# Inverting 16x16 triangular blocks on VectorE: substitution in blocks of 4 and two doublings in place of plain substitution

## The chip, the cores and the metric

The kernel runs on one core of one Trainium2 chip. The metric is the device time of one execution in microseconds (us), taken as the median of several executions. One further execution is recorded by the hardware profiler. Its engines are called PE (TensorE matmuls), PEld (TensorE weight loads), DVE (VectorE), ACT (ScalarE), POOL (GpSimd) and SP (the engine that issues most DMAs).

## What is computed

The reference is a two-layer decoder on 512 tokens of width 1024: a gated-DeltaNet layer, a differential-attention layer, and an MLP behind each. The change lies in the first layer's delta rule, which has 8 heads. For each head and chunk of tokens the reference does this:

```python
a_mat = where(strict, einsum('bhnik,bhnjk->bhnij', kb, kc) * decay, 0.0)   # strictly lower triangular
sol = triangular_solve(eye + a_mat, rhs, left_side=True, lower=True, unit_diagonal=True)
u, w = sol[..., :DV], sol[..., DV:]
...
v_new = u_i - w_i @ state          # step by step over the chunks
o_i = qg_i @ state + qk_i @ v_new
state = state * gl_i + kd_i.T @ v_new
```

What matters here is the inverse of a unit lower triangular matrix I + A, needed before the recurrence over the chunks can run.

## The kernel before, in words

The kernel computes the whole trunk in one program. Every large product is three fp32r matmuls on split operands (lines 300, 301 and 302 in `three`): weights are loaded as `raw`, ACT rounds them to `wh` (line 293), and DVE or POOL forms the remainder `wl` (line 284). During the delta-rule layer DVE forms `wl`; later POOL does.

The layer handles the heads in one Python loop. `proj_head(h)` does the projections of q, k and v on PE into three PSUM banks `pj` (their pool has three), and `conv_silu` empties each bank: one ACT pass (line 481) and three DVE passes (line 483). A bank is free for the next head's matmuls when the third pass has run. `gdn(h)` is a generator in three parts; the loop runs the first two parts of head h and then the last of head h-1.

The part that the change touches is in the first part of `gdn`. The head is worked in four units of 128 tokens. `bq` (line 558) holds the unit's triangular matrix and the attention weights. Lines 570 and 574 cut out the 16x16 diagonal blocks (8 in each unit, 32 in all) into `dc`. Two DMAs from SP (lines 576 and 578) bring them through DRAM into `mt`, which holds one block on each of 32 partitions, 256 numbers each, transposed: `mt[p, s, r]` is row r, column s. POOL sets `xv` to 32 unit matrices (line 581).

Then 15 steps of substitution follow. Step s takes column s of the block times the finished part of row s of the inverse into `pr` (line 584), and subtracts that from the rows below (line 586). Both are DVE instructions on (15 - s) x (s + 1) numbers on each of 32 partitions: 15, 28, 39, 48, 55, 60, 63, 64 and back down, 680 in all for each of the two lines, and each instruction needs the one before it. Two more DMAs (lines 589 and 591) bring the inverses back as `tc`; line 593 spreads them into the block-diagonal `t`; PE transposes `t` (line 598), and the inverse of the whole 128x128 matrix is completed by doubling from 16 to 32, 64 and 128 with matmuls on PE and copies and subtractions on DVE (lines 605 to 638). The recurrence (lines 670 to 690) needs that.

The order in which instructions stand on each engine is not the order of the program's text. The build fixes it for each engine, and mixes the steps of one head with the work of its neighbours; at run time each engine takes its queue strictly in that order, waiting on semaphores. While head h is being inverted, the convolutions of head h+1 or h+2, the `wl` remainders of coming weights, the recurrence of head h-1 and the modulation products of line 193 stand between its steps on DVE. After the last head come the output gates (`gate`, line 711 on), then the output projection.

Of the kernel before, what the change touches and what calls it, by code (L numbers as in the profile page):

```python
# [10 lines left out]
F32 = mybir.dt.float32  # L11
F32R = mybir.dt.float32r
AF = mybir.ActivationFunctionType
ALU = mybir.AluOpType
AX = mybir.AxisListType
# [5 lines left out]
S = 512  # L21
# [8 lines left out]
SUB = 16  # L30
# [55 lines left out]
def trunk_kernel(ctx: ExitStack, tc: tile.TileContext, a, outT):  # L86
    nc = tc.nc
    V, G, A, T = nc.vector, nc.gpsimd, nc.scalar, nc.tensor
# [3 lines left out]
    def nm(s):  # L92
        count[0] += 1
        return f"{s}_{count[0]}"

    def open_pool(name, side="left", bufs=1):
        st = ExitStack()
        p = st.enter_context(tc.tile_pool(name=nm(name), bufs=bufs, side=side, reuse_waits="tile"))
        return p, st
# [40 lines left out]
    def v3(ap, n=P):  # L140
        return ap.rearrange("p (u f) -> p u f", f=n)
# [286 lines left out]
    g_pool, g_st = open_pool("g", "right")  # L428
# [10 lines left out]
    def gt_(name):  # L439
# [18 lines left out]
                           op0=ALU.mult, op1=ALU.mult)  # L458
# [42 lines left out]
    def uu(t, n):  # L501
        return t[:, n * P:(n + 1) * P]

    def m4(ap):
        return ap.unsqueeze(1).to_broadcast([P, 4, P])

    m_sub = mask[:, M_L1:M_L1 + P]

    def gdn(h):
        def natural(src, tag="a"):  # L510
            ps = bank(tag)
            for c in range(NT):
                T.transpose(uu(ps, c), uu(src, c), ident)
            return ps
# [35 lines left out]
        for n in range(2):  # L550
# [5 lines left out]
            for c in (2 * n, 2 * n + 1):  # L556
                o = (c % 2) * 256
                V.scalar_tensor_tensor(out=v3(bq[n][:, o:o + 256]), in0=v3(ps[:, o:o + 256]), scalar=sj[:, c:c + 1],
                                       in1=uu(ex, c).unsqueeze(1).to_broadcast([P, 2, P]), op0=ALU.mult, op1=ALU.mult)
# [9 lines left out]
        for n in range(2):  # L569
            V.tensor_tensor(out=v3(db[:, n * 256:(n + 1) * 256]),  # L570
                            in0=bq[n].rearrange("p (u t f) -> p u t f", u=2, t=2)[:, :, 0, :],
                            in1=m_sub.unsqueeze(1).to_broadcast([P, 2, P]), op=ALU.mult)
# [4 lines left out]
        mt = g_pool.tile([32, SUB, SUB], F32, tag="mt", name=nm("mt"), bufs=2)  # L577
        nc.sync.dma_start(mt.rearrange("p r c -> p (r c)"), d1.rearrange("u (b r) c -> (u b) (r c)", r=SUB))
        xv = g_pool.tile([32, SUB, SUB], F32, tag="xv", name=nm("xv"), bufs=2)
        pr = g_pool.tile([32, SUB, SUB], F32, tag="pr", name=nm("pr"), bufs=2)  # L580
        G.tensor_copy(xv, eye)
        for s in range(SUB - 1):
            shp = [32, SUB - 1 - s, s + 1]
            V.tensor_tensor(out=pr[:, s + 1:, :s + 1], in0=mt[:, s, s + 1:].unsqueeze(2).to_broadcast(shp),
                            in1=xv[:, s, :s + 1].unsqueeze(1).to_broadcast(shp), op=ALU.mult)
            V.tensor_tensor(out=xv[:, s + 1:, :s + 1], in0=xv[:, s + 1:, :s + 1], in1=pr[:, s + 1:, :s + 1],
                            op=ALU.subtract)
        d2 = dp.tile([32, SUB * SUB], F32, tag="d2", name=nm("d2"))
        nc.sync.dma_start(d2, xv.rearrange("p r c -> p (r c)"))
        tc_ = g_pool.tile([P, 4, SUB], F32, tag="tc", name=nm("tc"), bufs=2)  # L590
# [3 lines left out]
                        in0=tc_.unsqueeze(2).to_broadcast([P, 4, P // SUB, SUB]),  # L594
                        in1=m4(m_sub).rearrange("p u (b c) -> p u b c", c=SUB), op=ALU.mult)
# [20 lines left out]
        for b in (32, 64):  # L616
# [13 lines left out]
            if b == 32:  # L630
                p0, p1 = parts[0]
                for n in range(4):
# [3 lines left out]
                                in1=v3(pz[p1, 0:4 * b], b), op=ALU.subtract)  # L636
            for p0, p1 in parts:
                V.tensor_tensor(out=v3(z)[p0, :, p1], in0=v3(z)[p0, :, p1], in1=v3(pz[p0, 0:4 * b], b),
                                op=ALU.subtract)
# [27 lines left out]
        for c in range(NT):  # L667
            r = uu(vn, 0)
            if c > 0:
# [3 lines left out]
                else:  # L673
# [3 lines left out]
                                       op0=ALU.mult, op1=ALU.add)  # L677
# [28 lines left out]
        else:  # L706
            V.scalar_tensor_tensor(out=oT[h], in0=natural(o, "r"), scalar=cc(C_OUTG), in1=sz[h],
                                   op0=ALU.mult, op1=ALU.mult)
# [20 lines left out]
    for h in range(H):  # L729
        proj_head(h)  # L730
        heads.append(gdn(h))
        next(heads[h])
        next(heads[h])
        if h:
            next(heads[h - 1], None)
# [50 lines left out]
    def after0(sl, rb):  # L786
        rbs.append(rb)
        for k in range(KT):
# [19 lines left out]
                           op0=ALU.add, op1=ALU.subtract)  # L808
# [202 lines left out]
```

## Time and profile before

| what | value |
|---|---|
| median of 3 runs | 1384.9 us (1381.57 to 1387.92) |
| the profiled execution | 1381.92 us, its span 1380.1 us, granted TensorE clock 0.986 |
| busy over the span | PE 1309.7 us, DVE 850.9 us, ACT 529.1 us, POOL 471.4 us |
| the inversions' stage, 100 to 346 us | PE 226.1 us of 246, DVE 221.6 us of 246 |
| lines 584 and 586 (15 of each in each of 8 heads) | 240 DVE instructions, first at 106.3 us, last at 346.0 us |

The profile is read as follows. Busy time counts an instruction's whole run, so neighbours in a pipelined engine overlap; the time that an instruction takes from its engine's queue is better read as the distance between its start and the next one's start. A timeline row that ends in "x2" holds two instructions. The granted clock is the share of full speed that the throttle allowed TensorE.

### The profile page before, as it was taken

What the parts mean: (1) busy time and instruction counts of PE and PEld (TensorE: products, weight loads), DVE (VectorE), ACT (ScalarE), POOL (GpSimd) and SP (SyncE); (2) the same over time, 40 slices, a digit from 0 to 9 for tenths busy, and PEclk for the clock granted to TensorE, in tenths of its full rate; (3) what the DMA queues carried; (4) which work ended last, traced back from release to release, by engine and by line L of the source; (5) the groups of instructions that cost most, each with busy time, mean ns of one, the idle gap of its engine ahead of it and who ended that gap; (6) DMA issues with size and microseconds to landing.
All of it is one profiled execution on the core that took longest, in us unless ns stands there. A gap on an engine that the chain in (4) does not pass through costs nothing. (4 is left out here: it accounts for less than half of the span.)

```text
span 1380.1 us, 19204 instructions
## 1 busy us (share of the span) xinstructions
PE 1309.7 (95%) x7240; PEld 1101.4 (80%) x7240; DVE 850.9 (62%) x1688; ACT 529.1 (38%) x951; POOL 471.4 (34%) x281
## 2 busy tenths in 40 slices
PE   4887998999999999999999999999999999999997
PEld 3665787777789888888888987888798888888886
DVE  6989899899846987778861687777552110031113
ACT  3394344443424533225332354444344322143221
POOL 3324132222004544444444012232135444444441
PEclk9997999999999999999999999999999999999998
DMA  9632223225542776776753233222113233233221
GB/s 314 212 90 57 81 78 81 74 72 147 175 151 65 266 239 225 242 236 219 241 165 100 81 100 104 65 66 66 61 62 123 92 96 103 92 100 99 92 76 62
DMA packets 113212, 174.97 MB, mean 127 GB/s; under 512 B 16384, under 2 KB 56992, under 8 KB 113120
## 3 DMA queue, kind: packets, MB, share of 16 engines
q1 hardware_dynamic: 112416, 172.92, 39.5%
q8 instruction: 57, 0.93, 0.3%
q10 hardware_dynamic: 704, 0.83, 0.2%
q14 instruction: 35, 0.29, 0.1%
HBM read 170.04 MB, written 2.62 MB: 125 GB/s over the span
## 5 line engine op out<-in xcount | busy, mean ns | idle before, releaser
L284 POOL TENSOR_TENSOR wl<-raw,wh 128x1024 fp32r<-128x1024 f32 (+1 forms) x137 | 329.3, 2404 | 392.9 <-ACT wh L293 392.9
L293 ACT ACTIVATE wh<-raw 128x1024 fp32r<-128x1024 f32 (+2 forms) x217 | 216.0, 996 | 502.0 <-PE pj L301 250.1
L300 PE MATMUL pj<-h,wh 128*128 128x512 f32 (+1 forms) x816 | 290.9, 360 | 16.0 <-ACT h L278 5.5
L301 PE MATMUL pj<-h,wh 128*128 128x512 f32 (+1 forms) x816 | 292.6, 359 | 0.0
L302 PE MATMUL pj<-h,wl 128*128 128x512 f32 (+1 forms) x816 | 290.4, 358 | 1.1 <-DVE wl L284 1.1
L193 DVE SCALAR_TENSOR_TENSOR mw<-mw,one,cs 128x1024 f32<-128x1024 f32 x96 | 210.1, 2202 | 47.5 <-ACT one L213 47.2
L300 PEld LDWEIGHTS pj<-h,wh 128*128 128x128 f32 x816 | 155.9, 192 | 37.2 <-ACT h L278 7.5
L302 PEld LDWEIGHTS pj<-h,wl 128*128 128x128 f32 x816 | 156.6, 192 | 19.4 <-DVE wl L284 2.4
L301 PEld LDWEIGHTS pj<-h,wh 128*128 128x128 f32 x816 | 156.9, 192 | 17.9 <-DVE h L279 0.3
L301 PE MATMUL pj<-u,wh 128*128 128x512 f32 (+1 forms) x448 | 160.9, 359 | 0.0
L302 PE MATMUL pj<-u,wl 128*128 128x512 f32 (+1 forms) x448 | 160.9, 359 | 0.0
L300 PE MATMUL pj<-u,wh 128*128 128x512 f32 (+1 forms) x448 | 160.8, 359 | 0.0
L346 DVE SCALAR_TENSOR_TENSOR x<-pj,mod,x 128x256 f32<-128x256 f32 (+1 forms) x53 | 30.2, 584 | 152.2 <-PE pj L302 152.2
L284 DVE TENSOR_TENSOR wl<-raw,wh 128x1024 fp32r<-128x1024 f32 (+2 forms) x80 | 84.5, 1058 | 18.7 <-ACT wh L293 18.6
L300 PEld LDWEIGHTS pj<-u,wh 128*128 128x128 f32 x448 | 84.6, 189 | 12.7 <-issue 0.2
L301 PEld LDWEIGHTS pj<-u,wh 128*128 128x128 f32 x448 | 84.6, 189 | 12.5
L302 PEld LDWEIGHTS pj<-u,wl 128*128 128x128 f32 x448 | 84.6, 189 | 12.5
L767 DVE SCALAR_TENSOR_TENSOR pj<-pj,r 128x512 f32<-128x512 f32 x32 | 21.6, 690 | 52.2 <-ACT r L766 52.0
L301 PE MATMUL pn<-h,wh 128*128 128x512 f32 x128 | 49.8, 389 | 0.0
L300 PE MATMUL pn<-h,wh 128*128 128x512 f32 x128 | 49.8, 389 | 0.0
L300 PE MATMUL pm<-h,wh 128*128 128x512 f32 x128 | 49.8, 389 | 0.0
L302 PE MATMUL pm<-h,wl 128*128 128x512 f32 x128 | 49.8, 389 | 0.0
(298 smaller groups left out, 2371.7 us busy)
## 6 DMA issues: line engine op xcount, KB each, us to landing
raw<-in_mlp_w_dram SPq DMA_DIRECT2D x128, 512.0 KB, 3.7
mw<-in_mod_wT_dram SPq DMA_DIRECT2D x96, 512.0 KB, 4.7
raw<-in_a_w_in_dram SPq DMA_DIRECT2D x96, 128.0 KB, 2.6
mw<-in_kv_mod_wT_dram SPq DMA_DIRECT2D x16, 512.0 KB, 5.1
raw<-in_kv_w_dram SPq DMA_DIRECT2D x16, 512.0 KB, 3.3
x<-in_xT_dram SPq DMA_DIRECT2D x16, 256.0 KB, 6.0
raw<-in_a_w_in_dram SPq DMA_DIRECT2D x16, 256.0 KB, 2.9
raw<-in_a_w_out_dram SPq DMA_DIRECT2D x8, 512.0 KB, 4.3
```

The source lines that it names most:

```text
L193: V.scalar_tensor_tensor(out=w, in0=w, scalar=one, in1=cs, op0=ALU.mult, op1=ALU.mult, accum_out=raw_mod[:, c:c + 1])
L284: (V if n else G).tensor_tensor(out=out, in0=x, in1=hi.bitcast(F32), op=ALU.subtract)
L293: A.activation(wh, raw, AF.Copy)
L300: T.matmul(ps, lhsT=wh, rhs=xh, start=first, stop=False, skip_group_check=skip)
L301: T.matmul(ps, lhsT=wh, rhs=xl, start=False, stop=False, skip_group_check=skip)
L302: T.matmul(ps, lhsT=wl, rhs=xh, start=False, stop=last, skip_group_check=skip)
L346: V.scalar_tensor_tensor(out=x[d][:, sl], in0=ps[j][:, sl], scalar=mod[:, gt + d:gt + d + 1], in1=x[d][:, sl], op0=ALU.mult, op1=ALU.add)
L767: V.scalar_tensor_tensor(out=ps[j], in0=ps[j], scalar=0.0, in1=r, op0=ALU.max, op1=ALU.mult)
```

## The change

`blocks_inv(mt, xv)` takes the place of the 15 steps. It first negates `mt` (one instruction on 256 numbers a partition). Substitution then runs on the four 4x4 diagonal blocks at once: three steps of two instructions, on 12, 16 and 12 numbers. Then pairs of neighbouring inverses are doubled, X21 = X22 (-M21) X11. Each of the two products in that is a multiply that writes all b x b x b terms into `pr`, and a reduction over the last axis. From 4 to 8 there are two such pairs, one after the other (64 terms each); from 8 to 16 there is one (512 terms). In all there are 1 + 6 + 8 + 4 = 19 instructions for 30. Each part needs the one before it. `pr` has one buffer of 512 numbers where it had two of 256, and a small tile `tq` is new.

```diff
+    def at(t, off, *dims):
+        v = t[:]
+        return bass.AP(tensor=v.tensor, offset=v.offset + off, ap=[list(v.ap[0])] + [list(d) for d in dims])
+
+    def blocks_inv(mt, xv):
+        V.tensor_scalar(out=mt, in0=mt, scalar1=-1.0, scalar2=None, op0=ALU.mult)
+        b, q = 4, 4 * (SUB + 1)
+        for i in range(b - 1):
+            m = b - 1 - i
+            pr = g_pool.tile([32, S], F32, tag="pr", name=nm("pr"), bufs=1)
+            prod, rest = at(pr, 0, (16, 4), (i + 1, m), (1, i + 1)), at(xv, (i + 1) * SUB, (q, 4), (SUB, m), (1, i + 1))
+            V.tensor_tensor(out=prod, in0=at(mt, i * SUB + i + 1, (q, 4), (1, m), (0, i + 1)),
+                            in1=at(xv, i * SUB, (q, 4), (0, m), (1, i + 1)), op=ALU.mult)
+            V.tensor_tensor(out=rest, in0=rest, in1=prod, op=ALU.add)
+        for b in (4, 8):
+            for lo in range(0, SUB, 2 * b):
+                d = lo * (SUB + 1)
+                pr = g_pool.tile([32, S], F32, tag="pr", name=nm("pr"), bufs=1)
+                tq = g_pool.tile([32, 64], F32, tag="tq", name=nm("tq"), bufs=1)
+                prod = at(pr, 0, (b * b, b), (b, b), (1, b))
+                V.tensor_tensor(out=prod, in0=at(mt, d + b, (1, b), (0, b), (SUB, b)),
+                                in1=at(xv, d, (0, b), (1, b), (SUB, b)), op=ALU.mult)
+                V.tensor_reduce(out=at(tq, 0, (b, b), (1, b)), in_=prod, axis=AX.X, op=ALU.add)
+                V.tensor_tensor(out=prod, in0=at(xv, d + b * (SUB + 1), (SUB, b), (0, b), (1, b)),
+                                in1=at(tq, 0, (0, b), (1, b), (b, b)), op=ALU.mult)
+                V.tensor_reduce(out=at(xv, d + b * SUB, (SUB, b), (1, b)), in_=prod, axis=AX.X, op=ALU.add)
...
-        pr = g_pool.tile([32, SUB, SUB], F32, tag="pr", name=nm("pr"), bufs=2)
         G.tensor_copy(xv, eye)
-        for s in range(SUB - 1):
-            shp = [32, SUB - 1 - s, s + 1]
-            V.tensor_tensor(out=pr[:, s + 1:, :s + 1], in0=mt[:, s, s + 1:].unsqueeze(2).to_broadcast(shp),
-                            in1=xv[:, s, :s + 1].unsqueeze(1).to_broadcast(shp), op=ALU.mult)
-            V.tensor_tensor(out=xv[:, s + 1:, :s + 1], in0=xv[:, s + 1:, :s + 1], in1=pr[:, s + 1:, :s + 1],
-                            op=ALU.subtract)
+        blocks_inv(mt, xv)
```

In the new text the four instructions of a doubling are lines 532 (multiply), 534 (reduce), 535 (multiply) and 537 (reduce); the negation is line 517, the small steps are lines 523 and 525. Lines behind the function have moved by 24, those of `gdn` ahead of the call by 30 (598 is now 622, 574 is now 604).

The change moves instructions on every engine, since the build lays out the order anew. The first place is DVE's queue at head 6 (the seventh). Before, the last third of its substitution stands between the next head's `bq` passes, single steps between single foreign instructions:

```order
L586 TENSOR_TENSOR xv_2810<-xv_2810,pr_2811 32x6x10
L558 SCALAR_TENSOR_TENSOR bq_3168<-pa_3176,sj_3164,ex_3147 128x256
L676 SCALAR_TENSOR_TENSOR r_2569<-pr_2560,neg,vn_2544 128x128
L584 TENSOR_TENSOR pr_2811<-mt_2808,xv_2810 32x5x11
L558 SCALAR_TENSOR_TENSOR bq_3168<-pa_3176,sj_3164,ex_3147 128x256
L586 TENSOR_TENSOR xv_2810<-xv_2810,pr_2811 32x5x11
L570 TENSOR_TENSOR db_3183<-bq_3167,mask 128x256
```

Now the same head's last doubling stands there, four long instructions between steps of head 5's recurrence (`st`, `o`, `r`, `y`):

```order
L532 TENSOR_TENSOR pr_2816<-mt_2790,xv_2792 32x512
L714 SCALAR_TENSOR_TENSOR st_2540<-st_2540,eg_all,pr_2542 128x128
L534 TENSOR_REDUCE tq_2817<-pr_2816 32x64
L550 TENSOR_REDUCE sqk_3138<-sqk_3136 128x4
L684 TENSOR_TENSOR o_2541<-o_2541,pr_2542 128x128
L700 SCALAR_TENSOR_TENSOR r_2575<-pr_2542,neg,vn_2526 128x128
L535 TENSOR_TENSOR pr_2816<-xv_2792,tq_2817 32x512
L571 TENSOR_SCALAR sqk_3138<-sqk_3138 128x4
L705 COPY y_2579<-pr_2542 128x128
L537 TENSOR_REDUCE xv_2792<-pr_2816 32x8x8
```

From a head's first to its last instruction on `xv` there were 66, 81, 110, 92, 89, 93, 84 and 75 rows of DVE's queue for heads 0 to 7; now there are 40, 46, 61, 60, 50, 53, 50 and 44.

The second place is PE's queue at the transposes of the same head's `t`. Before, they stand among the matmuls of an output gate, with the transposes of head 5's finished output (line 513) just ahead of them:

```order
L513 MATMUL pr_2614<-mask,o_2176 128x128 x4
L301 MATMUL pj_3474<-h_175,wh_3496 128x512
L302 MATMUL pj_3474<-h_174,wl_3498 128x512
L300 MATMUL pj_3475<-h_172,wh_3496 128x512
L598 MATMUL pi_2849<-mask,t_2847 128x128 x4
L605 MATMUL pi_2856<-t_2847,bq_2785 128x128 x2
```

Now they stand behind fewer matmuls, with transposes of the next head (line 543) ahead of them:

```order
L543 MATMUL pa_3286<-mask,cv_3104 128x128 x4
L301 MATMUL pj_3360<-h_183,wh_3423 128x512
L302 MATMUL pj_3360<-h_182,wl_3425 128x512
L300 MATMUL pj_3361<-h_180,wh_3423 128x512
L301 MATMUL pj_3361<-h_181,wh_3423 128x512
L622 MATMUL pi_2828<-mask,t_2826 128x128 x4
L629 MATMUL pi_2835<-t_2826,bq_2767 128x128 x2
```

Counted in projection matmuls that stand ahead of them on PE, the transposes of heads 0 to 7 stood behind 264, 312, 376, 460, 528, 611, 667 and 753; now they stand behind 280, 320, 339, 433, 519, 570, 645 and 728.

## Prediction

> **What bounds the kernel now.** I read the page first. Its engine line, and the rows that cut the span into 40 slices of 34.5 us, say that TensorE sets the time, and when VectorE is near its own limit:
>
> ```profile
> PE 1309.7 (95%) x7240; PEld 1101.4 (80%) x7240; DVE 850.9 (62%) x1688; ACT 529.1 (38%) x951; POOL 471.4 (34%) x281
> PE   4887998999999999999999999999999999999997
> DVE  6989899899846987778861687777552110031113
> PEclk9997999999999999999999999999999999999998
> ```
>
> PE is busy for 1309.7 of 1380.1 us. DVE's 62% is a mean: in slices 2 to 10, where the heads are inverted, its digits are 8 and 9, later 1 to 8. PE's digits of 8 lie there too. So I asked for the busy time of each engine by stretches of that stage (columns: stretch, its length, PE, PEld, DVE, ACT, POOL with instruction counts, granted clock, DMA share, GB/s):
>
> ```profile
> 100.00:140.00 40.00, 31.23 (x169) 24.66 (x168) 37.02 (x117) 19.15 (x34) 18.46 (x14) 0.75 0.25 60
> 140.00:220.00 80.00, 77.50 (x533) 63.05 (x533) 71.33 (x222) 36.36 (x63) 21.57 (x18) 1.00 0.28 77
> 220.00:300.00 80.00, 72.43 (x502) 59.62 (x503) 72.30 (x202) 37.75 (x68) 19.21 (x16) 0.98 0.29 79
> 300.00:346.00 46.00, 44.96 (x330) 35.85 (x329) 40.99 (x135) 13.65 (x29) 8.81 (x5) 1.00 0.44 123
> 346.00:380.00 34.00, 32.65 (x214) 25.91 (x213) 28.44 (x58) 14.99 (x29) 2.78 (x2) 1.00 0.59 180
> ```
>
> From 100 to 346 us PE is busy for 226.1 of 246 us and DVE for 221.6: two engines at about 90% that feed each other. PE is idle for 19.9 us, DVE for 24.4. Where DVE is fullest (93% of the first 40 us) PE is emptiest (8.8 us idle), and the granted clock is 0.75 there. The waits of PE in that stage, and those of DVE, name the direction (columns: total us, times, longest):
>
> ```profile
> PE pi L598 <- DVE t L593: 5.5, 4, 2.6
> PE pj L300 <- DVE cv L483: 4.5, 3, 2.6
> PE pj L300 <- DVE pr L584: 2.7, 1, 2.7
> ...
> DVE um L624 <- PE pi L622: 8.2, 11, 1.1
> DVE sj L545 <- POOL rk L543: 3.6, 7, 0.8
> ```
>
> PE waits for 12.7 of its 19.9 idle us in these three rows, all on DVE: for the spread inverses, and for PSUM banks that the convolutions empty late because they queue on DVE. DVE waits mostly for short round trips to PE.
>
> **The steps removed.** Three pieces of DVE's timeline give prices by the distance from one start to the next (start us, run us, what):
>
> ```profile
> 120.25 0.31 DVE L584 TENSOR_TENSOR pr<-mt,xv 32x60 f32<-32x60 f32 x2
> 120.50 0.31 DVE L586 TENSOR_TENSOR xv<-xv,pr 32x60 f32<-32x60 f32 x2
> 120.74 0.32 DVE L584 TENSOR_TENSOR pr<-mt,xv 32x55 f32<-32x55 f32 x2
> 120.98 0.32 DVE L586 TENSOR_TENSOR xv<-xv,pr 32x55 f32<-32x55 f32 x2
> 121.23 0.32 DVE L584 TENSOR_TENSOR pr<-mt,xv 32x48 f32<-32x48 f32 x2
> 121.47 0.32 DVE L586 TENSOR_TENSOR xv<-xv,pr 32x48 f32<-32x48 f32 x2
> 121.72 0.32 DVE L584 TENSOR_TENSOR pr<-mt,xv 32x39 f32<-32x39 f32 x2
> 121.96 0.32 DVE L586 TENSOR_TENSOR xv<-xv,pr 32x39 f32<-32x39 f32 x2
> 122.21 0.17 DVE L584 TENSOR_TENSOR pr<-mt,xv 32x28 f32<-32x28 f32 x1
> ```
>
> ```profile
> 284.73 0.16 DVE L586 TENSOR_TENSOR xv<-xv,pr 32x15 f32<-32x15 f32 x1
> 284.81 0.17 DVE L584 TENSOR_TENSOR pr<-mt,xv 32x15 f32<-32x15 f32 x1
> 284.89 0.67 DVE L284 TENSOR_TENSOR wl<-raw,wh 128x512 fp32r<-128x512 f32 x1
> ```
>
> ```profile
> 99.01 1.02 DVE L574 TENSOR_REDUCE dc<-db 128x64 f32<-128x512 f32 x1
> 99.96 0.67 DVE L520 TENSOR_REDUCE sqq<-sqk 128x4 f32<-128x512 f32 x1
> 100.55 0.73 DVE L483 SCALAR_TENSOR_TENSOR cv<-pj,cols,cv 128x511 f32<-128x511 f32 x1
> ```
>
> A step on 15 numbers takes 0.08 us of the queue, the plain reduction of 512 (line 520) takes 0.59. So a number costs (0.59 - 0.08)/497 = 1.03 ns, and an instruction 0.065 us besides. As a check, between 120.25 and 122.21 stand 16 steps on 60, 55, 48 and 39 numbers, 0.1225 us each, where the formula gives 0.117. A head's 30 steps with 1360 numbers cost 30 x 0.065 + 1.40 = 3.35 us, eight heads 26.8 us.
>
> **The steps added.** Line 574 is the useful row: it too reduces 512 to 64, reading with an innermost step of 16 numbers, and takes 0.95 us, 1.73 ns a number. The new multiplies read that way: line 532 steps by 16 in both inputs, line 535 by 4 or 8 in one. The new reductions read `pr` in sequence, as line 520 does.
> - Last doubling: two multiplies at 0.95, two reductions at 0.59: 3.08 us.
> - The two doublings from 4 to 8, 64 numbers an instruction: four multiplies at 0.065 + 64 x 1.73 ns = 0.176, four reductions at 0.131: 1.23 us.
> - Six small steps, 80 numbers: 0.39 + 0.08 = 0.47 us.
> - The negation of 256 numbers: no row shows a scalar operation of that size in SBUF. At 1.03 ns a number it is 0.33 us, at half of that 0.20. I take 0.33, the price that a row shows.
>
> That is 5.11 us, 1.76 us more than before in each head, 14.1 us more DVE time in eight. Fewer instructions, more numbers. Bounds: if the strides cost nothing and the negation takes 0.20, a head costs 4.08 us, +5.8 us in all. Upwards, line 532 may pay for both inputs: 0.70 ns more on 640 numbers is 0.45 us. And a DVE instruction can be held while POOL works, as this step on 63 numbers was, for about 0.8 us:
>
> ```profile
> 114.67 1.28 POOL L535 TENSOR_TENSOR ex<-ex,mask 128x512 f32<-128x512 f32 x1
> ```
>
> ```profile
> 114.98 1.04 DVE L584 TENSOR_TENSOR pr<-mt,xv 32x63 f32<-32x63 f32 x1
> ```
>
> Such holds happen to the old steps too. One more in every second head adds 0.4: 5.96 us a head, +21 us in all.
>
> The Trainium skill (Vector Engine (DVE) Microarchitecture Reference, section 5.2, Measured stream behaviour) says that a port runs at full rate only over runs of two or more neighbouring words, and gives 1.73 ns for one source that jumps at every element, but up to 2.50 ns where both step by 24 words. The 1.73 ns agrees with line 574 here; no run here shows two strided sources. By 2.50 ns line 532 would cost 0.49 us more a head, and the sum would be about +18 us of DVE time; my sum goes by line 574.
>
> **Order, buffers, queues.** The chain of one head now spans 40 to 61 rows of DVE's queue where it spanned 66 to 110, since 11 steps with their foreign neighbours are gone. PE's transposes of heads 2 to 7 stand 9 to 41 projection matmuls earlier, those of heads 0 and 1 stand 16 and 8 later. At most this removes the waits for `t` (5.5 us); of those I count 2, because each new place is again set for a DVE that is on time. The last head's earlier end is worth little: from 346 to 380 us PE lacks only 34 - 32.65 = 1.35 us, since gate matmuls cover that tail. SP issues the same four DMAs a head and POOL the same copy; nothing is added there. One `pr` buffer for two keeps two heads' chains apart; DVE takes its queue in order anyway, so I price that at nothing, the cover being the foreign instructions between the steps; without it a step would be exposed by about 0.17 - 0.08 = 0.09 us, 19 times, 1.7 us a head, within the upper end.
>
> **From DVE time to the span.** If nothing passed on, DVE would be busy for 235.7 of 246 us, 96%; the stretches above show PE idle 3% at 89% DVE, 9% at 90% and 22% at 93%. That speaks for a large share passing on; the 24.4 us of DVE idle speak for some being absorbed, though the larger waits in it are round trips that stay. I take 0.6 of 14.1, 8.5 us; the ends are 0 and 1. Idle PE also loses clock: (1 - 0.75) x 31.23 = 7.8 us in the first stretch, 1.4 us in the third; for 8.5 us more idle I add 1.5 us. The sum is 8.5 + 1.5 - 2 = +8.0 us. The profiled execution took 1381.9 us, its span and 1.8 us around it; that makes 1389.9. It lies 3.0 us below the median of the three runs, so the forecast for the median is 1393 us, 8 above 1384.9. A measurement of this kernel can tell about 0.5%, 6.9 us, from no change.
>
> **The rivals.**
> - *The count decides (faster).* The place is the hand-over from line 586 through `tc` and `t` to PE's line 598. If DVE's queue has room, a chain of 19 dependent steps ends sooner than one of 30, and PE's waits for `t` and for the bank behind line 584 go: 5.5 + 2.7 = 8.2 us, less a microsecond of new ones: 1378 us. It decides if the doublings cost no more queue time than the old steps, about 3.4 us a head. For it: those waits, and the fixed 0.065 us in 11 fewer instructions, 5.7 us over eight heads. Against it: 512 numbers cost 0.59 us even in sequence, four times a head. The Trainium skill (VectorE: DVE Perf Modes, section Rules for kernel authors) advises for chained DVE work to minimise the count of operations; by that rule the change should gain. The fixed part in the trace agrees, but the time for each number outweighs it here.
> - *Hidden (no change).* DVE's extra 14 us go into its own 24.4 us of idle, or into stretches where PE has work queued: at 140 to 220 us PE lacks only 2.5 of 80 us. 1381 to 1389 us. Against it: the third stretch, 7.6 us of PE idle with DVE no fuller.
> - *All of it shows (slower).* The whole of 14 to 21 us comes out on PE, through convolutions (line 483) and `wl` (line 284) standing behind multiplies of a microsecond: 1399 to 1406 us.
>
> **How the numbers follow.** The forecast with a share of 0.4 to 0.8, +5 to +11 us or 1390 to 1396: 0.40, three quarters of it above 6.9 us. Count decides: 0.13, nearly all beyond 0.5%. Hidden: 0.29. All of it: 0.18. Faster 0.12, same 0.10 + 0.29 + 0.01 = 0.40, slower 0.30 + 0.18 = 0.48. The range runs from the rival that gains, with 2 us to spare, to the full price: 1376 to 1406.
>
> **What would show it.** In the changed profile, line 532 and line 535 on 512 numbers should run about 1.02 us, lines 534 and 537 0.67, the group over 5 us of queue a head; DVE in the stage should be above 92%, and PE's waits for `cv` and `wl` should grow. The forecast is wrong if the strided multiplies run at 0.67, if DVE's busy share falls, or if PE's idle in the stage stays near 20 us.

## The result, and the profile after

The changed kernel takes 1396.4 us (median of 4 runs), the kernel before 1384.3 us beside it: ratio 1.0081, 95% interval 1.0055 to 1.0108. It is slower by 12.1 us; the forecast was 8 us slower, range 1376 to 1406. (Microseconds are differences of medians; ratios and intervals are worked out over all runs, and the two can differ by 0.1% of the time.) The profiled execution took 1393.8 us, its span is 1391.9 us, 11.8 us longer than before. The same rows of its page as were read before:

```profile
PE 1315.0 (94%) x7240; PEld 1103.0 (79%) x7240; DVE 862.7 (62%) x1600; ACT 529.7 (38%) x951; POOL 470.0 (34%) x281
PE   4888899989999999999999999999999999999997
DVE  6979888998875887778881577777552110031113
PEclk9998999999999999999999999999999999999998
```

DVE runs 88 instructions fewer and is busy 11.8 us longer. PE is busy 5.3 us longer for the same 7240 matmuls, and idle for 76.9 us where it was idle for 70.4: the 11.8 us are 6.5 us of idle PE and 5.3 us of longer busy time. The granted clock explains part of the second: 0.986 of a span of 1380.1 us loses 19.3 us, 0.984 of 1391.9 us loses 22.3, so about 3.0 of the 5.3 us; the rest is not explained. The stretches show where (columns as in the prediction):

```profile
100.00:140.00 40.00, 32.89 (x186) 25.77 (x186) 38.86 (x97) 19.96 (x36) 18.00 (x15) 0.83 0.25 63
140.00:220.00 80.00, 70.39 (x476) 55.61 (x475) 69.80 (x178) 30.93 (x56) 17.86 (x15) 0.96 0.27 71
220.00:300.00 80.00, 73.70 (x492) 59.40 (x492) 73.45 (x178) 35.41 (x62) 23.57 (x20) 0.96 0.24 66
300.00:346.00 46.00, 41.99 (x309) 33.32 (x309) 40.55 (x106) 15.87 (x30) 7.15 (x6) 0.96 0.29 80
...
380.00:420.00 40.00, 37.97 (x201) 31.88 (x200) 28.57 (x50) 17.55 (x29) 3.28 (x2) 1.00 0.65 213
```

The loss lies from 140 to 220 us (PE idle 9.6 us, 2.5 before) and from 300 to 346 (4.0, was 1.0); in both the granted clock fell from 1.00 to 0.96. The first stretch became better (7.1 us idle, clock 0.83), and from 220 to 300 us PE is idle for 6.3 us, was 7.6. Over the four stretches from 100 to 346 us that is 27.0 us of idle PE for 19.9. The last row shows that the end of the layer did not suffer.

The groups of DVE instructions by shape, with busy time and mean ns of one, show the new prices:

```profile
L535 DVE TENSOR_TENSOR pr<-xv,tq 32x512 f32<-32x512 f32 x8 | 8.9, 1117 | 0.0
L532 DVE TENSOR_TENSOR pr<-mt,xv 32x512 f32<-32x512 f32 x8 | 8.8, 1098 | 0.1
...
L534 DVE TENSOR_REDUCE tq<-pr 32x64 f32<-32x512 f32 x8 | 5.3, 665 | 0.0
L537 DVE TENSOR_REDUCE xv<-pr 32x64 f32<-32x512 f32 x8 | 5.3, 665 | 0.0
```

A piece of DVE's timeline in head 0, the negation of head 1 and the last doubling, gives them as distances from start to start:

```profile
117.73 0.27 DVE L517 TENSOR_SCALAR mt<-mt 32x256 f32<-32x256 f32 x1
117.93 1.02 DVE L532 TENSOR_TENSOR pr<-mt,xv 32x512 f32<-32x512 f32 x1
118.88 0.15 DVE L571 TENSOR_SCALAR sqk<-sqk 128x4 f32<-128x4 f32 x1
...
120.95 1.08 DVE L535 TENSOR_TENSOR pr<-xv,tq 32x512 f32<-32x512 f32 x1
121.95 0.14 DVE L576 TENSOR_TENSOR sj<-sj,beta 128x4 f32<-128x4 f32 x1
...
122.90 0.67 DVE L537 TENSOR_REDUCE xv<-pr 32x64 f32<-32x512 f32 x1
123.49 0.46 DVE L588 SCALAR_TENSOR_TENSOR bq<-pa,sj,ex 128x256 f32<-128x256 f32 x1
```

Negation 0.20 us, line 532 0.95, line 535 1.00, line 537 0.59.

PE's waits from 90 to 365 us, first of the changed kernel:

```profile
PE pi L622 <- DVE t L617: 5.0, 3, 2.8
PE pj L300 <- DVE cv L483: 4.8, 4, 3.5
PE pa L543 <- DVE bq L588: 3.3, 4, 2.4
PE pr L694 <- DVE st L712: 2.8, 3, 2.0
PE pj L302 <- DVE wl L284: 2.2, 4, 0.9
...
PE pr L707 <- DVE y L705: 1.4, 3, 0.7
...
PE pr L702 <- DVE r L700: 1.2, 2, 1.0
```

Then the rows of the kernel before that answer to the smaller of these:

```profile
PE pr L670 <- DVE st L690: 1.3, 2, 0.8
PE pa L513 <- DVE bq L558: 1.1, 2, 0.9
...
PE pj L302 <- DVE wl L284: 0.8, 2, 0.6
...
PE pr L683 <- DVE y L681: 0.2, 1, 0.2
```

The waits for the inverse (`t`) and for the convolutions (`cv`) are about what they were: for `t` one more, of 1.4 us, lies just behind the window, at 365.6 us, so they are 6.4 us in four where they were 5.5 in four. The wait of 2.7 us for a bank behind line 584 is gone. Longer became the waits inside the recurrence (`st`, `y`, `r`: 5.4 us, were 1.5), for `bq` (3.3, was 1.1) and for `wl` (2.2, was 0.8). One of them can be watched. DVE's queue around 168 us, where a multiply of 512 numbers, held to 1.61 us there, stands ahead of the recurrence's `st`:

```profile
167.20 1.61 DVE L532 TENSOR_TENSOR pr<-mt,xv 32x512 f32<-32x512 f32 x1
168.74 0.27 DVE L712 COPY st<-pr 128x128 f32<-128x128 f32 x1
```

and PE's next instruction:

```profile
169.07 0.49 PE L694 MATMUL pr<-st,cv 128*128 128x128 f32 x2 [2.01 <-DVE st L712]
```

### The profile page after: what moved, and what is told of

Same layout as the page of the kernel before. It is cut to its first block, busy times and chain, and to the rows that moved or that the text cites. A ratio compares the mean times of both kernels' runs of the same rounds, so it can differ in the third digit from the quotient of the medians.

```text
span 1391.9 us, 19105 instructions
## 1 busy us (share of the span) xinstructions
PE 1315.0 (94%) x7240; PEld 1103.0 (79%) x7240; DVE 862.7 (62%) x1600; ACT 529.7 (38%) x951; POOL 470.0 (34%) x281
## 5 line engine op out<-in xcount | busy, mean ns | idle before, releaser
L302 PEld LDWEIGHTS pj<-h,wl 128*128 128x128 f32 x816 | 156.6, 193 | 22.3 <-DVE wl L284 4.3
L300 PEld LDWEIGHTS pj<-u,wh 128*128 128x128 f32 x448 | 84.6, 189 | 12.7 <-issue 0.2
L302 PE MATMUL pn<-h,wl 128*128 128x512 f32 x128 | 49.8, 389 | 0.0
```

What stands on the lines that cost most here:

```text
L300: T.matmul(ps, lhsT=wh, rhs=xh, start=first, stop=False, skip_group_check=skip)
L302: T.matmul(ps, lhsT=wl, rhs=xh, start=False, stop=last, skip_group_check=skip)
```

## The experiments

Theory D is the prediction's: DVE's queue time is the cause, and most of it comes out. Theory O: the build's new order costs by itself, whatever DVE's load. Theory C: the length of the chain of dependent steps counts. Each run below was timed in five rounds beside the kernel before, and is compared with the runs of the kernel before that were timed with it.

**The changed kernel once more** (no edit).

> The changed kernel once more, beside the next three kernels on one chip. Both theories expect the ratio found, 1.0081, within about 0.25%: 1.006 to 1.010. It is the mark for the run that reads in sequence.

Measured 1.0074 (1.0059 to 1.0090), 11.4 us slower; its profile has DVE busy for 863.6 us and PE for 1315.3. The result stands.

**Read in sequence.** The order of the changed kernel, with less time in two of its instructions:

```diff
-V.tensor_tensor(out=prod, in0=at(mt, d + b, (1, b), (0, b), (SUB, b)),
-                in1=at(xv, d, (0, b), (1, b), (SUB, b)), op=ALU.mult)
+V.tensor_tensor(out=prod, in0=at(mt, d + b, (SUB, b), (0, b), (1, b)),
+                in1=at(xv, d, (0, b), (SUB, b), (1, b)), op=ALU.mult)
...
-                in1=at(tq, 0, (0, b), (1, b), (b, b)), op=ALU.mult)
+                in1=at(tq, 0, (0, b), (b, b), (1, b)), op=ALU.mult)
```

> The changed kernel with every operand of the doublings read in sequence (lines 532 and 535 then multiply other numbers than the inverse needs). The order of instructions on all five engines is the same, row for row. DVE's queue should lose 0.36 + 0.41 us in the last doubling and about 0.1 in each of the two doublings before it, 0.98 us a head, 7.8 us in all. Theory D (DVE's queue time is the cause, 0.6 to 1.0 of it comes out): 4.7 to 7.8 us less than the changed kernel, ratio to the kernel before 1.003 to 1.0055. Theory O (the new layout of the order costs, whatever DVE's load): no change, 1.006 to 1.010.

Measured 1.0029 (1.0016 to 1.0043), 5.5 us slower than before and 5.9 us faster than the changed kernel beside it; the two intervals do not meet. In its DVE timeline the two multiplies now take 0.60 us:

```profile
117.00 0.67 DVE L532 TENSOR_TENSOR pr<-mt,xv 32x512 f32<-32x512 f32 x1
117.60 0.15 DVE L571 TENSOR_SCALAR sqk<-sqk 128x4 f32<-128x4 f32 x1
...
119.67 0.67 DVE L535 TENSOR_TENSOR pr<-xv,tq 32x512 f32<-32x512 f32 x1
120.27 0.15 DVE L576 TENSOR_TENSOR sj<-sj,beta 128x4 f32<-128x4 f32 x1
```

DVE's total fell by 8.6 us, to 855.0, at one and the same order of instructions; 5.9 of them came out, a share of 0.7. PE was busy as long as in the changed kernel (1315.5 us, was 1315.3): the gain is idle time alone. Theory O falls as an explanation of half the loss. The reads with a stride are that half.

**Strided before.** The order of the kernel before, with more time in its steps:

```diff
-shp = [32, SUB - 1 - s, s + 1]
-V.tensor_tensor(out=pr[:, s + 1:, :s + 1], in0=mt[:, s, s + 1:].unsqueeze(2).to_broadcast(shp),
-                in1=xv[:, s, :s + 1].unsqueeze(1).to_broadcast(shp), op=ALU.mult)
-V.tensor_tensor(out=xv[:, s + 1:, :s + 1], in0=xv[:, s + 1:, :s + 1], in1=pr[:, s + 1:, :s + 1],
-                op=ALU.subtract)
+shp = [32, s + 1, SUB - 1 - s]
+pt, xt = pr.rearrange("p r c -> p c r"), xv.rearrange("p r c -> p c r")
+V.tensor_tensor(out=pt[:, :s + 1, s + 1:], in0=mt[:, s, s + 1:].unsqueeze(1).to_broadcast(shp),
+                in1=xv[:, s, :s + 1].unsqueeze(2).to_broadcast(shp), op=ALU.mult)
+V.tensor_tensor(out=xt[:, :s + 1, s + 1:], in0=xt[:, :s + 1, s + 1:], in1=pt[:, :s + 1, s + 1:],
+                op=ALU.subtract)
```

> The kernel before with the two loops of each substitution step exchanged, so that the inner loop runs down the rows: line 584 writes with a step of 16 numbers, line 586 reads and writes so in all operands. The result and the order of instructions on all five engines are those of the kernel before. At 0.7 ns more on 680 numbers of line 584 and 1.0 to 1.5 ns more on 680 of line 586, DVE's queue should gain 1.2 to 1.5 us a head, 9 to 12 us in all. Theory D: 5.5 to 12 us slower, ratio 1.004 to 1.009. Theory O: the same order, so no change, 0.998 to 1.002.

Measured 1.0005 (0.9994 to 1.0015): no change, as Theory O had it. But the edit did not do what was expected of it. Its two groups:

```profile
L585 DVE TENSOR_TENSOR pr<-mt,xv 32x15 f32<-32x15 f32 (+7 forms) x120 | 29.0, 252 | 0.3
...
L587 DVE TENSOR_TENSOR xv<-xv,pr 32x15 f32<-32x15 f32 (+7 forms) x120 | 28.2, 242 | 0.3
```

They were busy 57.2 us where lines 584 and 586 were busy 50.9 (26.5 and 24.4), and DVE's total rose by 2.6 us only, to 853.5. A dose of 2.6 us cannot be told from nothing here, so the run decides nothing.

**More DVE work off the chain.**

```diff
+            if s == 7:
+                dm = g_pool.tile([32, 12, SUB], F32, tag="dm", name=nm("dm"), bufs=1)
+                for _ in range(7):
+                    V.tensor_tensor(out=dm, in0=eye[:, :12], in1=eye[:, :12], op=ALU.mult)
```

> The kernel before with seven more DVE multiplies of 192 numbers in each head, into a tile that nobody reads: 7 x (0.065 + 0.198) = 1.84 us of DVE's queue a head, 14.7 us in all, with no step added to the chain of the inverse. The build lays out the order anew for it. Theory D: 9 to 15 us slower, ratio 1.0065 to 1.011. Theory C (what counts is how many dependent steps the chain has, the load of DVE being absorbed): no change, 0.997 to 1.003. Theory O: any ratio, since the order is another one.

Measured 1.0105 (1.0088 to 1.0121), 16.0 us slower, with DVE busy 16.8 us longer (867.7). The inverse's chain has no step more, and the time follows the load all the same. PE's waits for `t` are even shorter than before, 3.7 us for 5.5; those for `wl` grew from 0.8 to 9.5. That tells against Theory C's claim that the load is absorbed, and agrees with D.

**Two chains.**

```diff
+        pp = [g_pool.tile([32, 64], F32, tag=f"pp{n}", name=nm("pp"), bufs=2) for n in range(2)]
+        x2 = g_pool.tile([32, SUB, SUB], F32, tag="x2", name=nm("x2"), bufs=1)
         G.tensor_copy(xv, eye)
+        G.tensor_copy(x2, eye)
...
+            xw = (x2, xv)[s % 2]
+            pq = pp[s % 2][:, :shp[1] * shp[2]].rearrange("p (a b) -> p a b", b=s + 1)
```

(The step's two instructions then use `xw` and `pq` for `xv` and `pr`.)

> The kernel before with its 15 steps dealt out to two chains that don't need each other: odd steps work on the inverse, even steps on a second tile that nobody reads (so the inverse is not complete). The same 30 instructions on the same numbers, but no more than 15 or 16 of them in a row depend on each other; one more copy by POOL a head. Theory C (the length of the chain counts): PE's waits for the inverses shrink, 2 to 8 us faster, 0.994 to 0.9985. Theory D: DVE's queue time is the same, so 0.9985 to 1.003.

Measured 1.0033 (1.0021 to 1.0045), 4.4 us slower, with DVE's total 2.0 us lower. The build moved the transposes of `t` earlier (head 7's stand behind 680 projection matmuls where they stood behind 753). PE's waits for the inverses did shrink, as Theory C said, to 1.9 us from 5.5, but the convolutions paid, as PE's largest wait shows (4.5 us before):

```profile
PE pj L300 <- DVE cv L483: 12.6, 4, 4.0
...
PE pi L601 <- DVE t L596: 1.9, 1, 1.9
```

So the shorter chain gained nothing on balance, but whether it gains at an unchanged order is not shown. D's bound of 1.003 is just passed: an order of its own, the extra copies by POOL, or the single buffer of the second tile (`x2`) cost some 4 us here, and this run does not part them.

**To 8 only.**

```diff
-        for b in (4, 8):
+        for b in (4,):
```

> The changed kernel without the doubling from 8 to 16: the lower left 8x8 quarter of each inverse stays zero, so it computes less than the reference needs. 15 instructions a head. Against the changed kernel DVE's queue loses 0.95 + 1.00 + 0.59 + 0.59 = 3.13 us a head, 25 us in all; against the kernel before it loses about 11. Theory D: faster than the kernel before by 4 to 9 us, as far as PE has idle time to give, ratio 0.9935 to 0.997. Theory O: the order is another new one, 1.004 to 1.010 like the changed kernel's.

Measured 0.9866 (0.9850 to 0.9883), 19.0 us faster than before, twice what Theory D gave. But DVE's total fell by more than was worked out, too: it is 832.7 us, 18.2 below the kernel before where 11 were expected. Time followed it one for one, below the old load as well. The four instructions of the doubling from 8 to 16 are where the loss lies: with them 1396, without them, and without that quarter of the inverse, 1365 us.

**The sums of squares to ACT**, in the kernel before and in the changed one.

```diff
-            A.activation(sq, src, AF.Square)
             ss = col(4, tag)
-            V.tensor_reduce(out=ss, in_=v3(sq), axis=AX.X, op=ALU.add)
+            for c in range(NT):
+                A.activation(uu(sq, c), uu(src, c), AF.Square, accum_out=ss[:, c:c + 1])
```

> The kernel before with the 24 reductions of squares (line 520, 0.59 us of DVE's queue each) taken to ACT: four squares of 128 with an accumulated sum in place of one of 512. DVE's queue loses 14 us in the stage, ACT gains some 20 of its 139 idle us there. The inversion is untouched. Theory D: 6 to 12 us faster, 0.991 to 0.996. If PE itself bounds the stage and DVE's load is only seen where it exceeds that of the kernel before: no change, 0.998 to 1.002.

Measured 0.9862 (0.9845 to 0.9878): 1364.8 us, 19.4 us faster than the kernel before, for 14.2 us of DVE time (836.7), and more than the 6 to 12 us of Theory D. Its stretches:

```profile
100.00:140.00 40.00, 33.02 (x191) 26.07 (x189) 38.20 (x120) 20.70 (x61) 18.47 (x11) 0.83 0.41 106
140.00:220.00 80.00, 76.92 (x542) 62.78 (x540) 72.24 (x218) 46.21 (x124) 23.52 (x21) 1.00 0.29 78
220.00:300.00 80.00, 78.24 (x582) 63.92 (x582) 73.28 (x229) 40.35 (x123) 19.32 (x18) 1.00 0.27 75
```

From 220 to 300 us PE lacks 1.8 us where it lacked 7.6. PE is busy for 1302.0 us in all, 7.7 less than in the kernel before for the same matmuls; the granted clock, 0.991 for 0.986, accounts for about 7.0 of that. The edit also takes a reduction out of the chain ahead of `bq`, and lays out another order; this run does not part these from DVE's load.

> The changed kernel with the same 24 reductions taken to ACT. Its DVE total then is about that of the kernel before. Theory D: the gain of the run before it, set against the loss of the change, 0.997 to 1.002; the change still costs about 8 to 12 us against the kernel before with the same edit. If only load above some level costs, the change is nearly free here: the same ratio as the run before it, within 0.3%.

Measured 0.9975 (0.9962 to 0.9987): 1380.6 us, 15.9 us behind the kernel before with the same edit, and DVE's total is 846.0, 9.3 us above that one's. At the lower load the change costs no less: 15.9 us where 8 to 12 were expected, 1.7 us for each us of DVE, so DVE's load alone does not account for it. PE's waits for `t`, first with the change, then without it, show one place:

```profile
PE pi L622 <- DVE t L617: 5.3, 3, 2.1
```

```profile
PE pi L598 <- DVE t L593: 0.7, 2, 0.4
```

Down to that load the change's DVE time was not free.

**A new order alone.** Lines 641 to 653 (`nk`, `kd`, `kn`, `vn`, `ssq`, `rq`) written ahead of `db = big(g_pool, "db", 1)`, nothing else.

> The kernel before with the part of the head that follows the inverse and does not need it (the normalisation and transposes of k, v and q, lines 641 to 653) written ahead of the inversion. The same instructions on the same numbers; the build lays out another order on every engine. Theory D (time follows DVE's busy total): the same, 0.997 to 1.003. Theory O (the change's loss is the price of a new order): 1.004 to 1.010, as the changed kernel's new order.

Measured 1.0014 (1.0001 to 1.0026), 1.4 us slower, with DVE's total 1.3 us higher. This new order with the old work is nearly free, which tells against Theory O. It is one order; the run with one buffer, below, is another with the same instructions, and that one costs 16.4 us.

**More copies to ACT**, on top of the sums in the kernel before.

```diff
-                V.tensor_copy(um[p1, 0:4 * b], pu[p1, 0:4 * b])
+                A.activation(um[p1, 0:4 * b], pu[p1, 0:4 * b], AF.Copy)
```

> The kernel before with the sums of squares on ACT, and the 24 copies of line 624 (PSUM to SBUF, in the doubling on PE) on ACT too: some 7 us of DVE less again. Theory D: 0.979 to 0.984. If PE has no idle time left to give: 0.986 as without the second edit. If ACT's copies are late for PE: 0.988 to 0.995.

Measured 0.9852 (0.9838 to 0.9865). It cannot be told from the sums alone, and Theory D's range is missed; but DVE's total fell by only 1.8 us further, to 834.9, where 7 were expected.

```diff
-            V.tensor_copy(y, R(2))
+            A.activation(y, R(2), AF.Copy)
```

> As the run before it, with the 32 copies of line 681 (the recurrence's y, PSUM to SBUF) on ACT as well: 6 to 7 us of DVE less again. Theory D: 0.974 to 0.980. The rival is the recurrence's own chain: a copy on ACT takes some 0.37 us where DVE took 0.28, 32 times in a chain of dependent steps, and the time would rise again by up to 3 us: 0.982 to 0.986.

Measured 0.9906 (0.9892 to 0.9919): 12.9 us faster than the kernel before, but 7 us slower than without this edit, with DVE's total at 829.1, the lowest of all. Here the time does not follow DVE; both expectations missed. The copy itself took no longer on ACT (0.28 us, as on DVE, where 0.37 was expected), and no wait of PE for `y` stands among those listed; PE's waits for `t` (3.3 us) and `bq` (3.4 us) are there, and were not in the run without this edit. What brought them is open.

**One buffer for `pr`** in the kernel before (`bufs=2` to `bufs=1` on line 580).

> The kernel before with one buffer for the products of a step where it has two, as the change has. The steps of two heads can then not stand mixed in DVE's queue; the instructions are the same. If the single buffer is part of the change's price: 1.002 to 1.008. Theory D (DVE's busy total, which stays): 0.998 to 1.002.

Measured 1.0109 (1.0092 to 1.0126): 16.4 us slower, with DVE's total only 2.9 us higher. This is more than either expectation. The instructions are the same; the order on every engine is new. The largest part of the loss lies at the end of the layer, first in this run, then in the kernel before:

```profile
380.00:420.00 40.00, 29.25 (x169) 22.23 (x169) 17.02 (x38) 5.78 (x11) 2.80 (x3) 0.74 0.24 80
```

```profile
380.00:420.00 40.00, 37.16 (x230) 32.58 (x230) 20.11 (x37) 11.80 (x19) 3.60 (x3) 0.96 0.37 126
```

With one buffer the steps of two heads cannot mix, each head's chain starts when the last has ended, and head 7's transposes slip from behind 753 projection matmuls to behind 842. The gates end at 792, so they stand in the output projection, which needs head 7: PE is idle for 10.8 of 40 us (was 2.8), and the clock falls to 0.74. Over the whole span PE is idle for 11.8 us more than before, 7.9 of them in this stretch.

All runs against DVE's total (differences to the kernel before, in us; DVE busy from one profile of each, time by the medians):

| run | DVE busy | time |
|---|---|---|
| strided before | +2.6 | +1.3 |
| a new order alone | +1.3 | +1.4 |
| read in sequence | +4.1 | +5.5 |
| changed kernel, again | +12.7 | +11.4 |
| more DVE work | +16.8 | +16.0 |
| sums to ACT, changed kernel | -4.9 | -3.6 |
| sums to ACT, kernel before | -14.2 | -19.4 |
| sums and `um` to ACT | -16.0 | -20.2 |
| to 8 only | -18.2 | -19.0 |
| two chains | -2.0 | +4.4 |
| one buffer for `pr` | +2.9 | +16.4 |
| sums, `um` and `y` to ACT | -21.8 | -12.9 |

Nine rows follow DVE's total within about 5 us. The last three do not. Two of them change a buffer or the chain, the third a queue of the recurrence; that this sets them apart is a reading after the fact, not shown by itself.

## Why the prediction was right, and where it was not

The direction and the reason were right: more time on DVE's queue, read from rows of the trace, and most of it coming out on PE. The size, 12.1 us for 8, came out larger by one term of the sum.

- **The price of the steps was right.** Forecast 5.11 us of queue a head. From start to start it is 0.20 + 6 x 0.08 + 0.95 + 1.00 + 2 x 0.59 = 3.81 for all but the doublings to 8; those take 0.18, 0.13, 0.19 and 0.12 us, twice, 1.24: 5.05 us. The row of line 574, a reduction with the same step, gave the price of a strided multiply exactly. The upper bound for line 532, paying for both strided inputs, did not come: 0.95 us is 1.73 ns a number. The Trainium skill's 2.50 ns (Vector Engine (DVE) Microarchitecture Reference, section 5.2), given for steps of 24 words, does not hold for two sources that step by 16 numbers; the measurement decides. The negation took the lower of the two prices considered, 0.20 us.
- **DVE's gain in load was about right:** +14.1 us forecast, +11.8 and +12.7 us busy in two profiles. DVE's share of the stage did not pass 92%, as it should have: it is busy for 222.7 of the 246 us, 90.5%, and was 90.1% before. The extra time stretched the stage instead; the last of the new steps starts at 357.3 us, where the last old one started at 346.0.
- **The idle of PE was right in sum, not in its parts.** 8.5 - 2 = 6.5 us forecast, 6.5 measured, and 8.1 in the second profile: that it met to the tenth is luck. The 2 us off the waits for `t` did not come (6.4 us, was 5.5): head 7's transposes stand 25 projection matmuls earlier in the order, but their `t` is made at 363.6 us where it was made at 354.8.
- **PE's longer busy time was the term mis-sized.** It was forecast at +1.5 us, as loss of clock from more idle; PE's busy time rose by 5.3 us, from 1309.7 to 1315.0, and by 5.6 in the second profile. The step that failed was to size this term by the third stretch alone (1.4 us lost for 7.6 us idle); stretches that ran at 1.00 before run at 0.96 now. By the granted clock the loss is about 3.0 us in the first profile (worked out above) and 1.6 in the second (0.985 of 1393.8 us), so as a loss of clock alone the term was up to twice too small; where the other 2 to 4 us come from stays open. With 5.3 for 1.5 the sum is +11.8.
- **The waits came elsewhere.** The prediction looked to convolutions and `wl`; they grew by 0.3 and 1.4 us, the recurrence's waits by 3.9 and `bq`'s by 2.2. The place can be seen in the order shown ahead of the prediction: the four long instructions stand between `st`, `r` and `y`.
- **The single buffer was priced at nothing, for the wrong reason.** DVE's fixed order is no cover for it, as its own run shows (+16.4 us). In the changed kernel the chain itself is the cover: it is so much shorter that head 7's transposes stand behind 728 projection matmuls instead of 842. That reading rests on the two orders and on the undisturbed last stretch; the changed kernel with two buffers was not tried.
- **The rivals.** "The count decides" fell: 19 instructions cost more than 30. The rule to minimise the count of chained operations (the Trainium skill, VectorE: DVE Perf Modes, section Rules for kernel authors) does not hold here; 11 fixed parts of 0.065 us a head were saved, and 2896 numbers stand in place of 1360, part of them read with a stride. "Hidden" fell too: with the sums off DVE the change cost 15.9 us still. "All of it shows" is nearest in kind: in the pairs of runs that follow DVE's load by more than a few us, its time comes out at 0.7 (read in sequence) to 1.7 (the change with the sums on ACT) for one, where 0.6 was taken.
- **What is shown, and what is not.** For half of the loss, the reads with a stride, the cause is shown at an unchanged order. The other half, 5.5 us at +4.1 us of DVE, agrees with DVE's load, but the new order and the single buffer came with it and were not taken apart from it in the changed kernel.

## What to carry to other kernels

Price a rewrite of small vector steps by queue time, so much for an instruction and so much for a number, with its own price for strided reads taken from the nearest strided row; the count alone misleads. Where two engines feed each other at 90%, load on the second can come out in full, as it did here in both directions (0.7 to 1.7 us for each us), so the better edit here was to take 14 us of plain reductions off DVE (ratio 0.9862), not to rearrange the inverse. And a buffer's count can hold up the last link of a chain far from where it stands.

## What the runs showed that was not expected

- PE's idle time can cost busy time too, but at no fixed rate: 14.2 us taken off DVE made PE idle 10.5 us less and busy 7.7 us less, about 7.0 of that by the granted clock; in the changed kernel +6.5 us idle went with +5.3 us busy; and reading in sequence, against the second profile of the changed kernel, took off 4.5 us of idle and nothing of the busy time.
- The DVE steps with all three operands strided by 16 numbers cost no more than those with one. On 64 numbers the run rose from 0.205 to 0.253 us, 0.75 ns a number; line 574 pays 0.70.
- On ACT a square of 128 numbers with an accumulated sum took two records, the second a read of the accumulator; two of the groups of ACT in the kernel before with the sums there:

```profile
L520 ACT ACTIVATE sqk<-pa 128x128 f32<-128x128 f32 x32 | 8.4, 278 | 7.7 <-PE pa L513 7.4
...
L520 ACT ACTIVATION_READ_ACCUMULATOR sqk<-pa 128x1 f32 x32 | 6.6, 207 | 0.0
```
